# Four edits to a two-block transformer kernel: load order, a split residual tile, a shifted norm, wider convolution matmuls

## The chip, the cores and the metric

The kernel runs on one core of one Trainium2 chip. The metric is the device time of one execution in microseconds (us), the median of several executions. Lower is better. Engines are named as the profile names them: PE (TensorE matmul), PEld (TensorE weight load), DVE (VectorE), ACT (ScalarE), POOL (GpSimd), SP (SyncE, which here only issues DMAs).

## What is computed

Two blocks of two layers each work on 256 tokens of width 1024 in float32. In the first block a layer is a mixer (gated linear attention beside retention) and a feed-forward part (a SwiGLU of width 2816, then eight experts). In the second block a context of 256 further tokens runs beside the first 256. Its first layer is SwiGLU, short convolution, SwiGLU; its second is SwiGLU, latent attention, SwiGLU. Every part is preceded by an RMS norm that is scaled and shifted by "modulations", which are products of a condition vector with large matrices:

```python
def rms_norm_2(x, g):
    y = x * rsqrt(mean(x * x, axis=-1) + EPS)
    return y * g

def pre(h, g, shift, scale):
    return rms_norm_2(h, g) * (1 + scale) + shift

def adaln_chunks(cond, w_mod, b_mod):              # 9 vectors of 1024 (6 in the first block)
    return split(silu(cond) @ w_mod + b_mod, N_MOD)

def short_conv_mixer(h, w_in, conv_w, w_out):      # 3 taps along the tokens, centred
    b_gate, c_gate, u = split(h @ w_in, 3, axis=-1)
    return (b_gate * conv3_centred(c_gate * u, conv_w)) @ w_out
```

In the second block's first layer the convolution runs on the 256 tokens and on the 256 of the context, so on 512 columns.

## The kernel before, in words

**Layout and precision.** Activations stand transposed: 128 rows of the width on the partitions, eight such blocks (KD = 8), tokens along the free axis. Every float32 product is made of three matmuls on parts `hi` and `lo` of both operands (`dot_w`, lines 523 to 527: hi·hi at L525, lo·hi at L526, hi·lo at L527). The residual stream is the tile `H`, 128 x 8 x 512: columns 0 to 255 are the tokens, 256 to 511 the context.

**The stream of loads.** Class `Stream` (line 44) plans everything that SP loads through five buffers of 1 MB (tile `raw`, 128 x 2048). A *weight unit* (DRAM tensor `in_wts`) is loaded, cast to `whi` by ACT (L117), and DVE subtracts to get `wlo` (L121). There are three pairs of those, and a unit is split up to two steps ahead of the step that multiplies with it. A *modulation unit* (DRAM tensor `in_modt`) is not split: at its own step DVE multiplies it by the condition vector and sums each row (`column`, L280, two halves of 1024 columns, each once or, in the second block's first five vectors, twice). Steps run in program order, and every engine works its queue strictly in the order in which the steps were written. The order of the loads is a list of its own, `seq`; a unit that is appended with `after=n` is put into that list only behind the next n weight units. In the kernel before all units have n = 0, so the loads stand in the order of the steps.

`act` (line 329) appends a weight step and, by a rate that is set for each part, calls `fill`, which appends one modulation step ahead of it:

```python
key, src, fn = queue.pop(0)
S.step([(src, False)], fn)
```

The rate is 0.75 in the first mixer, 0.88 in the first feed-forward part (`ffn_a`), 0 in the experts, and between 0.45 and 0.8 later.

**The start.** SP loads the tokens (L1909), then modulation units 0 to 2, two weight units, and units 3 to 7. ACT squares the eight blocks of `H` and PE sums them (`first_stats`); DVE takes the inverse root. The first norm's scale and shift arrive in eight pieces, one for each block k: `cols(k)` is two columns and a small operation that makes `A` (L801). `go(k)` then has ACT scale the block (L816) and cast it to `ahi` (L817), DVE make `alo` (L818), and PE multiply block k by the first two weight units.

**The convolution.** For each quarter m2 of the width, `conv` multiplies by three units `c`, `u` and `b` of 256 columns. `products` runs over blocks kc, token halves h and column blocks j, so each matmul has 256 token columns; the accumulator is one bank for each half h. The first `c` and `u` (m2 = 0) are interleaved with the norm's blocks and run a half at a time. The evacuation (`out_c`, `out_u`, `out_b`) works by halves too.

Of the kernel before, what the change touches and what calls it, by code (L numbers as in the profile page):

```python
# [208 lines left out]
def body(ctx: ExitStack, tc: tile.TileContext, A: dict, out: bass.AP):  # L209
# [107 lines left out]
    def fill(n):  # L317
        for _ in range(min(n, len(queue))):
            while queue[0][1] is None:
                S.step([], queue.pop(0)[2])  # L320
            key, src, fn = queue.pop(0)
            S.step([(src, False)], fn)

    def need(key):

# [15 lines left out]
        S.step([], fn)  # L341


    H = cst.tile([128, KD, 512], F32, name="H")

    def rsqrt_ops(ms, n):

# [37 lines left out]
    class Stat:  # L385


        def __init__(self, off):
            self.off = off
            self.s = slice(off, off + TOK)  # L390
            self.pend = self.R = None

        def add(self, m):
            src = H[:, m, self.s]
# [42 lines left out]
        def modulate(self, hi, lo, a, b):  # L437

            def finish(m, t):
                nc.scalar.activation(hi[:, m, self.s], t, AF.Identity, bias=b[:, m:m + 1])  # L440
                nc.vector.scalar_tensor_tensor(lo[:, m, self.s], t, b[:, m:m + 1], hi[:, m, self.s].bitcast(F32),
                                               op0=OP.add, op1=OP.subtract)

            ts = []
            for m in range(KD):
                t = T()[:, :TOK]
                nc.vector.scalar_tensor_tensor(t, H[:, m, self.s], a[:, m:m + 1], self.R[:, :TOK], op0=OP.mult, op1=OP.mult)
                ts.append(t)
                if m == 0:
                    finish(0, t)  # L450
                    yield 0
                elif m > 1:
                    finish(m - 1, ts[m - 1])
                    yield m - 1
            finish(KD - 1, ts[KD - 1])
            yield KD - 1

    class Final(Stat):
# [8 lines left out]
        def add(self, m):  # L467
            for scale in (1.0, vc("final_g", m)):
                sq = T()[:, :TOK]
                nc.scalar.activation(sq, H[:, m, self.s], AF.Square, scale=scale)  # L470
                self.sq.append(sq)

        def take(self):
# [31 lines left out]

        def done(self):
            for m in range(KD):
                nc.vector.scalar_tensor_tensor(H[:, m, self.s], H[:, m, self.s], vc("final_g", m), self.acc2,
                                               op0=OP.mult, op1=OP.mult)

    def scale_cols(key, g, sc):
# [221 lines left out]
    def resid_of(gates, stats, final=False):  # L733

        def resid(m, o, h, last=True):
            g = gates()
            for i in (range(len(g)) if h is None else [h]):
                src = o[:, half(i)] if h is None else o
                d = H[:, m, half(i)]
                nc.vector.scalar_tensor_tensor(d, src, g[i][:, m:m + 1], d, op0=OP.mult, op1=OP.add)  # L740
                if last and stats is not None:
                    stats[i].add(m)
                elif last and final:
                    nc.sync.dma_start(out[:, m], d)
        return resid


    def mixer(l, s_in, ab, resid):
# [41 lines left out]
        if l == 0:  # L790
# [14 lines left out]
            def normed(a, b):  # L805
                if a == 0:
                    xs[0] = P["p"].tile([128, 1536], F32, name="S")
                    xs[1] = P["p"].tile([128, 512], F32, name="la")
                for k in range(a, b):
                    v = xs["v", k] = xs[k // 6][:, (k % 6) * 256:(k % 6) * 256 + 256]  # L810
                    nc.vector.tensor_mul(v, H[:, k, 0:TOK], s_in.R[:, :TOK])
# [8 lines left out]
            def cols_step(j, then=None):  # L820
                def fn(raw):
                    cols(j)(raw)
                    if then is not None:
                        then()
                S.step([(A["modt"][j].rearrange("p (a b) -> p a b", a=2), False)], fn)

            def start(pa, pq):
                xs["w"] = pa, pq
                for k in range(3):
                    chunk(k)  # L830
                first_products(pa, pq, range(3))

            def go(k):
                chunk(k)
                first_products(*xs["w"], [k])
                if k == KD - 1:
                    S.free(2)
                    S.ahead(2)
                    first_out()
# [944 lines left out]
    def conv(stats, ab, resid, hook):  # L1784
# [14 lines left out]
        for m2 in range(4):  # L1799
            hold = {}  # L1800

            def products(nm, part, hs, kcs, hold=hold):
                whi, wlo = part
                for kc in kcs:
                    for h in hs:
                        for j in range(2):
                            dot_w(hold[nm, h][:, half(j)], whi[:, kc, blk(j)], wlo[:, kc, blk(j)],
                                  st["a"][0][:, kc, half(h)], st["a"][1][:, kc, half(h)],
                                  first=(kc == 0 and j == 0), last=(kc == KD - 1))

            def alloc(nm, hold=hold):
                for h in range(2):
                    hold[nm, h] = bank()

            def out_c(hold=hold):
                for h in range(2):
                    hold["cs", h] = T()
                    nc.scalar.copy(hold["cs", h], hold["c", h])

            def out_u(m2=m2, hold=hold):  # L1820
                for h in range(2):
                    cu = m["cu"][h]
                    nc.vector.tensor_mul(cu[:, :, 1:257], hold["cs", h].rearrange("p (j t) -> p j t", j=2),
                                         hold["u", h].rearrange("p (j t) -> p j t", j=2))
                    y = hold["y", h] = T()
                    for j in range(2):
                        v = y[:, half(j)]
                        wc = lambda tap: vc("sc_conv_2", tap * 8 + 2 * m2 + j)
                        nc.scalar.activation(v, cu[:, j, 1:257], AF.Copy, scale=wc(1))
                        nc.vector.scalar_tensor_tensor(v, cu[:, j, 0:256], wc(0), v, op0=OP.mult, op1=OP.add)  # L1830
                        nc.vector.scalar_tensor_tensor(v, cu[:, j, 2:258], wc(2), v, op0=OP.mult, op1=OP.add)

            def out_b(m2=m2, hold=hold):
                for h in range(2):
                    y = hold["y", h]
                    nc.vector.tensor_mul(y, y, hold["b", h])
                    split_to(st["g"][0][:, 2 * m2:2 * m2 + 2, half(h)], st["g"][1][:, 2 * m2:2 * m2 + 2, half(h)],
                             y.rearrange("p (j t) -> p j t", j=2))

            def unit(nm, m2=m2):  # L1840
                c0 = {"b": 0, "c": D, "u": 2 * D}[nm] + m2 * 256
# [2 lines left out]
            if m2 == 0:  # L1844
                def fn(pc_, pu, alloc=alloc, products=products, out_c=out_c, out_u=out_u):
# [2 lines left out]

                    def mm_half(h, kcs):
                        for kc in kcs:  # L1850
                            products("c", pc_, [h], [kc])
                            products("u", pu, [h], [kc])
                    entry_of(st, stats, ab)(mm_half)
                    out_c()
                    out_u()
# [1 line left out]
            else:  # L1857
                def fc(part, alloc=alloc, products=products, out_c=out_c):
                    alloc("c")
                    products("c", part, range(2), range(KD))  # L1860
                    out_c()

                def fu(part, alloc=alloc, products=products, out_u=out_u):
                    alloc("u")
                    products("u", part, range(2), range(KD))
                    out_u()
                act([unit("c")], fc)
                act([unit("u")], fu)

            def fb(part, alloc=alloc, products=products, out_b=out_b):  # L1870
                alloc("b")
                products("b", part, range(2), range(KD))
# [33 lines left out]
        return hook  # L1906


    nc.sync.dma_start(H[:, :, 0:TOK], A["xt"])  # L1909
    s_a = Stat(0)  # L1910

    def first_stats():
        s_a.p = tbank()
        for k in range(KD):
            sq = T()[:, :TOK]
            nc.scalar.activation(sq, H[:, k, 0:TOK], AF.Square)
# [228 lines left out]
```

## Time and profile before

| What | Value |
|---|---|
| Median of three runs | 2718.47 us (2715.21 to 2720.2) |
| The profiled execution's own time | 2725.84 us |
| Its span | 2724.0 us, 36201 instructions |
| PE busy | 2578.3 us (95%) |
| DVE busy | 1806.8 us (66%) |
| ACT busy | 1088.1 us (40%) |
| DMA | 511.46 MB, mean 188 GB/s |
| Chain that ended last | PE 73% of the span, in lines L525 to L527 alone 54% |

The span runs from the first to the last instruction; 1.84 us of the execution's time lie outside it. The profiled execution was 7.4 us (0.27%) longer than the median of the runs. A matmul's duration in the trace includes a pipeline's depth, so consecutive matmuls overlap in it: how fast they follow each other is read from their starts.

### The profile page before, as it was taken

How to read it: one execution, taken by the hardware profiler on the slowest of the kernel's cores; microseconds unless marked ns; L12 is line 12 of the kernel's file. 1: busy time of each engine (PE TensorE's matmuls, PEld its weight loads, DVE VectorE, ACT ScalarE, POOL GpSimd, SP SyncE). 2: the span in 40 equal slices, each digit the busy share in tenths (PEclk: the TensorE clock that was granted, in tenths of full speed). 3: DMA queues.
4: the chain of work that ended last, by engine and by line, in shares of the span. 5: the costliest groups of instructions: out<-in, count | busy, mean ns of one | idle time of the engine just before them, and what ended most of it. 6: DMA issues, size and time to landing. Idle time of an engine off the chain costs nothing.

```text
span 2724.0 us, 36201 instructions
## 1 busy us (share of the span) xinstructions
PE 2578.3 (95%) x15060; PEld 2277.0 (84%) x15060; DVE 1806.8 (66%) x2477; ACT 1088.1 (40%) x1214; POOL 25.9 (1%) x40
## 2 busy tenths in 40 slices
PE   5988998978999999999999999999999999999999
PEld 4778987777888888888889998888888888876999
DVE  5867777776888886655558766555476654555653
ACT  3433335346777775222223233222232122345442
POOL 0100000000000000000000000000000000000000
PEclk6999998888999999999999999999999999999999
DMA  7655886435988984343333423443324554202442
GB/s 297 232 201 219 309 316 251 167 140 208 342 335 329 350 331 176 141 167 133 126 144 125 170 109 139 153 149 135 136 109 166 201 190 176 79 32 78 173 177 100
DMA packets 77297, 511.46 MB, mean 188 GB/s; under 512 B 8498, under 2 KB 11860, under 8 KB 23236
## 3 DMA queue, kind: packets, MB, share of 16 engines
q1 hardware_dynamic: 76020, 506.27, 50.2%
q8 instruction: 120, 1.97, 0.3%
q0 software_dynamic: 672, 2.00, 0.2%
q10 hardware_dynamic: 432, 0.79, 0.1%
q14 instruction: 53, 0.43, 0.1%
HBM read 507.97 MB, written 1.05 MB: 187 GB/s over the span
## 4 chain that ended last, share of the span: by engine, by line
PE 73%; DVE 2%; ACT 1%; issue 1%; DVEq 0%; ACTq 0%
PE acc L526 18%; PE acc L525 18%; PE acc L527 18%; PE acc L532 4%; PE acc L533 4%; PE acc L531 4%; DVE wlo L121 1%; PE acc L1742 1%; PE acc L1715 1%; ACT whi L117 1%; PE acc L1319 1%; PE acc L1331 1%; PE acc L1714 0%; PE tb L1360 0%; DVE accs L401 0%
## 5 line engine op out<-in xcount | busy, mean ns | idle before, releaser
L121 DVE TENSOR_TENSOR wlo<-raw,whi 128x2048 fp32r<-128x2048 f32 (+3 forms) x385 | 818.9, 2133 | 449.5 <-ACT whi L117 448.8
L117 ACT CAST whi<-raw 128x2048 fp32r<-128x2048 f32 (+3 forms) x387 | 686.8, 1782 | 718.2 <-PE acc L526 309.2
L525 PE MATMUL acc<-ahi,whi 128*128 128x256 f32 (+1 forms) x2624 | 859.0, 327 | 17.2 <-ACT ahi L817 11.5
L527 PE MATMUL acc<-ahi,wlo 128*128 128x256 f32 (+1 forms) x2624 | 855.6, 326 | 11.6 <-DVE wlo L121 11.6
L526 PE MATMUL acc<-alo,whi 128*128 128x256 f32 (+1 forms) x2624 | 857.1, 327 | 6.3 <-DVE alo L818 5.5
L525 PEld LDWEIGHTS acc<-ahi,whi 128*128 128x128 f32 x2624 | 510.1, 194 | 59.4 <-ACT ahi L817 12.8
L527 PEld LDWEIGHTS acc<-ahi,wlo 128*128 128x128 f32 x2624 | 509.8, 194 | 51.5 <-DVE wlo L121 14.0
L526 PEld LDWEIGHTS acc<-alo,whi 128*128 128x128 f32 x2624 | 510.0, 194 | 47.1 <-DVE alo L818 6.6
L526 PE MATMUL acc<-glo,whi 128*128 128x256 f32 (+1 forms) x1076 | 346.9, 322 | 0.0
L527 PE MATMUL acc<-ghi,wlo 128*128 128x256 f32 (+1 forms) x1044 | 338.7, 324 | 6.3 <-DVE wlo L121 6.2
L525 PE MATMUL acc<-ghi,whi 128*128 128x256 f32 (+1 forms) x1044 | 338.8, 324 | 0.0
L280 DVE CUSTOM_DVE_ANT_0 raw<-raw,cond,vec 128x1024 f32<-128x1024 f32 x240 | 303.8, 1286 | 15.6 <-DMA raw<-in_modt_dram 11.5
L527 PEld LDWEIGHTS acc<-ghi,wlo 128*128 128x128 f32 x1044 | 199.1, 191 | 23.4 <-DVE wlo L121 7.9
L526 PEld LDWEIGHTS acc<-glo,whi 128*128 128x128 f32 x1076 | 205.1, 191 | 15.6
L525 PEld LDWEIGHTS acc<-ghi,whi 128*128 128x128 f32 x1044 | 199.2, 191 | 15.6
L536 ACT CAST ghi<-T 128x512 fp32r<-128x512 f32 x88 | 54.7, 622 | 339.6 <-DVE T L610 339.6
L610 DVE TENSOR_TENSOR T<-T,acc 128x512 f32<-128x512 f32 x88 | 60.3, 685 | 153.8 <-PE acc L527 153.8
L531 PE MATMUL acc<-whi,xg 128*128 128x512 f32 (+1 forms) x384 | 145.9, 380 | 0.0
L280 DVE CUSTOM_DVE_ANT_0 T<-raw,cond,vec 128x1024 bf16<-128x1024 f32 x112 | 143.3, 1280 | 1.7 <-ACT cond L269 1.7
L533 PE MATMUL acc<-whi,xg 128*128 128x512 f32 (+1 forms) x384 | 144.4, 376 | 0.0
L532 PE MATMUL acc<-wlo,xg 128*128 128x512 f32 (+1 forms) x384 | 144.3, 376 | 0.0
L537 DVE TENSOR_TENSOR glo<-T,ghi 128x512 fp32r<-128x512 f32 x88 | 60.9, 692 | 60.5 <-ACT ghi L536 60.5
(370 smaller groups left out, 2432.7 us busy)
## 6 DMA issues: line engine op xcount, KB each, us to landing
raw<-in_wts_dram SPq DMA_DIRECT2D x300, 1024.0 KB, 5.0
raw<-in_modt_dram SPq DMA_DIRECT2D x120, 1024.0 KB, 4.8
raw<-in_wts_dram SPq DMA_DIRECT2D x60, 768.0 KB, 4.6
raw<-in_wts_dram SPq DMA_DIRECT2D x18, 512.0 KB, 3.7
raw<-in_wts_dram SPq DMA_DIRECT2D x2, 896.0 KB, 5.4
dec<-in_consts_dram SPq DMA_DIRECT2D x2, 768.0 KB, 6.7
raw<-in_mla_w_uq_dram SPq DMA_DIRECT2D x2, 768.0 KB, 4.2
H<-in_xt_dram SPq DMA_DIRECT2D x1, 1024.0 KB, 9.1
```

The source lines that it names most:

```text
L117: nc.scalar.copy(hd, sv)
L121: nc.vector.tensor_sub(ld, sv, hd.bitcast(F32))
L280: nc.vector.tensor_tensor_reduce(w if last else T().bitcast(mybir.dt.bfloat16), w, cond, 1.0, bias, OP.mult, OP.add, out)
L525: mm(o, whi, xhi, start=first, stop=False, skip_group_check=True)
L526: mm(o, whi, xlo, start=False, stop=False, skip_group_check=True)
L527: mm(o, wlo, xhi, start=False, stop=last, skip_group_check=True)
L531: mm(o, xhi, whi, start=first, stop=False, skip_group_check=True)
L532: mm(o, xhi, wlo, start=False, stop=False, skip_group_check=True)
L533: mm(o, xlo, whi, start=False, stop=last, skip_group_check=True)
L536: nc.scalar.copy(hi, v)
L537: nc.vector.tensor_sub(lo, v, hi.bitcast(F32))
L610: nc.vector.tensor_mul(v, s, b3[:, :n])
```

## The change

Four things are edited.

1. `fill` appends modulation units with `after=2`: each is loaded behind two weight units that are used after it. The step itself stays where it was.
2. `H` becomes two tiles of 128 x 8 x 256, one for the tokens and one for the context. All uses are renamed; the two loads that fill them are now written in one run of 2048 columns for each partition instead of eight runs of 256.
3. In the first norm `alo` and the products of block k - 1 (`use`) are written behind the scaling and cast of block k.
4. In `conv`, `products` runs over column blocks j, then blocks kc, with all 512 token columns in one matmul (except for the first `c` and `u`). An accumulator bank now belongs to a column block j, and the evacuation works by j.

```diff
@@ fill
-            S.step([(src, False)], fn)
+            S.step([(src, False)], fn, after=2)
...
-    H = cst.tile([128, KD, 512], F32, name="H")
+    H = [cst.tile([128, KD, TOK], F32, name=f"H{i}") for i in range(2)]
...
@@ mixer, first norm
             def chunk(k):
-                t = T()[:, :TOK]
-                hi, lo = st["a"][0][:, k], st["a"][1][:, k]
+                t = xs["t", k] = T()[:, :TOK]
                 nc.scalar.activation(t, xs["v", k], AF.Identity, scale=A_[:, k:k + 1], bias=sh[:, k:k + 1])
-                nc.scalar.copy(hi, t)
-                nc.vector.tensor_sub(lo, t, hi.bitcast(F32))
+                nc.scalar.copy(st["a"][0][:, k], t)
+
+            def use(k):
+                nc.vector.tensor_sub(st["a"][1][:, k], xs["t", k], st["a"][0][:, k].bitcast(F32))
+                first_products(*xs["w"], [k])
...
                 for k in range(3):
                     chunk(k)
-                first_products(pa, pq, range(3))
+                for k in range(2):
+                    use(k)
             def go(k):
                 chunk(k)
-                first_products(*xs["w"], [k])
+                use(k - 1)
                 if k == KD - 1:
+                    use(k)
                     S.free(2)
...
@@ conv
-                for kc in kcs:
-                    for h in hs:
-                        for j in range(2):
-                            dot_w(hold[nm, h][:, half(j)], whi[:, kc, blk(j)], wlo[:, kc, blk(j)],
-                                  st["a"][0][:, kc, half(h)], st["a"][1][:, kc, half(h)],
-                                  first=(kc == 0 and j == 0), last=(kc == KD - 1))
+                for j in range(2):
+                    for kc in kcs:
+                        dot_w(hold[nm, j][:, toks], whi[:, kc, blk(j)], wlo[:, kc, blk(j)],
+                              st["a"][0][:, kc, toks], st["a"][1][:, kc, toks],
+                              first=(kc == 0 and toks.start == 0), last=(kc == KD - 1))
...
-                    for j in range(2):
-                        v = y[:, half(j)]
-                        wc = lambda tap: vc("sc_conv_2", tap * 8 + 2 * m2 + j)
-                        nc.scalar.activation(v, cu[:, j, 1:257], AF.Copy, scale=wc(1))
-                        nc.vector.scalar_tensor_tensor(v, cu[:, j, 0:256], wc(0), v, op0=OP.mult, op1=OP.add)
-                        nc.vector.scalar_tensor_tensor(v, cu[:, j, 2:258], wc(2), v, op0=OP.mult, op1=OP.add)
+                    v = y.rearrange("p (h t) -> p h t", h=2)
+                    wc = lambda tap: vc("sc_conv_2", tap * 8 + 2 * m2 + j)
+                    nc.scalar.activation(v, cu[:, :, 1:257], AF.Copy, scale=wc(1))
+                    nc.vector.scalar_tensor_tensor(v, cu[:, :, 0:256], wc(0), v, op0=OP.mult, op1=OP.add)
+                    nc.vector.scalar_tensor_tensor(v, cu[:, :, 2:258], wc(2), v, op0=OP.mult, op1=OP.add)
...
-                            products("c", pc_, [h], [kc])
+                            products("c", pc_, half(h), [kc])
...
-                    products("c", part, range(2), range(KD))
+                    products("c", part, slice(0, 512), range(KD))
...
-    nc.sync.dma_start(H[:, :, 0:TOK], A["xt"])
+    nc.sync.dma_start(H[0], A["xt"])
...
-        nc.sync.dma_start(H[:, :, TOK:2 * TOK], A["ctxt"])
+        nc.sync.dma_start(H[1], A["ctxt"])
```

**SP's loads as `ffn_a` begins.** Before (the number in a name only tells tiles apart):

```order
L97 DMA raw_1723<-in_wts_dram 128x2048
L97 DMA raw_1725<-in_modt_dram 128x2048
L97 DMA raw_1782<-in_wts_dram 128x2048
L97 DMA raw_1784<-in_modt_dram 128x2048
L97 DMA raw_1847<-in_wts_dram 128x2048
L97 DMA raw_1849<-in_modt_dram 128x2048
L97 DMA raw_1906<-in_wts_dram 128x2048
```

DVE, in the same place before, takes those buffers in this order (the rows between are other operations):

```order
L121 TENSOR_TENSOR wlo_1852<-raw_1847,whi_1851 128x2048
L280 ISA raw_1725,mod1_0_5_1720<-raw_1725,cond0_76,vec_86 128x1024
L121 TENSOR_TENSOR wlo_1911<-raw_1906,whi_1910 128x2048
L280 ISA raw_1784,mod1_1_0_1969<-raw_1784,cond0_76,vec_86 128x1024
L121 TENSOR_TENSOR wlo_1977<-raw_1972,whi_1976 128x2048
```

So the modulation unit `raw_1725`, loaded ahead of the weights `raw_1782` and `raw_1847`, is used up behind `raw_1847`. With the change, SP loads:

```order
L97 DMA raw_1711<-in_wts_dram 128x2048
L97 DMA raw_1717<-in_modt_dram 128x2048
L97 DMA raw_1732<-in_wts_dram 128x2048
L97 DMA raw_1734<-in_modt_dram 128x2048
L97 DMA raw_1787<-in_wts_dram 128x2048
L97 DMA raw_1793<-in_modt_dram 128x2048
L97 DMA raw_1852<-in_wts_dram 128x2048
```

and DVE uses them in this order:

```order
L121 TENSOR_TENSOR wlo_1790<-raw_1711,whi_1789 128x2048
L280 ISA raw_1717,mod1_0_5_1729<-raw_1717,cond0_76,vec_86 128x1024
L121 TENSOR_TENSOR wlo_1855<-raw_1732,whi_1854 128x2048
L280 ISA raw_1734,mod1_0_5_1729<-raw_1734,cond0_76,vec_86 128x1024
L121 TENSOR_TENSOR wlo_1914<-raw_1787,whi_1913 128x2048
L280 ISA raw_1793,mod1_1_0_1974<-raw_1793,cond0_76,vec_86 128x1024
L121 TENSOR_TENSOR wlo_1980<-raw_1852,whi_1979 128x2048
```

DVE's work stands in the same order as before, apart from three weight subtractions in the whole program that come a few rows earlier; the loads now stand in the order in which DVE gives their buffers back. In the whole program each modulation unit that `fill` appends (units 8 to 119) stands two weight units later in SP's list.

**DVE in the first norm.** Before, around block 3 (`T_251` is that block):

```order
L280 ISA raw_173,mod1_0_1_93<-raw_173,cond0_76,vec_86 128x1024
L280 ISA mod1_0_1_93 128x1
L801 SCALAR_TENSOR_TENSOR A_100_94<-mod1_0_1_93,vec_86 128x1
L818 TENSOR_TENSOR alo_110<-T_251,ahi_109 128x256
L280 ISA raw_184,mod1_0_0_92<-raw_184,cond0_76,vec_86 128x1024
```

With the change (`T_214` is block 2):

```order
L280 ISA raw_174,mod1_0_1_94<-raw_174,cond0_76,vec_86 128x1024
L280 ISA mod1_0_1_94 128x1
L803 SCALAR_TENSOR_TENSOR A_100_95<-mod1_0_1_94,vec_86 128x1
L822 TENSOR_TENSOR alo_111<-T_214,ahi_110 128x256
L280 ISA raw_185,mod1_0_0_93<-raw_185,cond0_76,vec_86 128x1024
```

The `alo` behind the columns of block 3 is that of block 2.

## Rows read from the trace of the kernel before

**Rows 1.** Page part 1: busy time, share of the span and instructions of each engine.

```profile
PE 2578.3 (95%) x15060; PEld 2277.0 (84%) x15060; DVE 1806.8 (66%) x2477; ACT 1088.1 (40%) x1214; POOL 25.9 (1%) x40
```

**Rows 2.** Windows by stage: first mixer, `ffn_a`, convolution (columns in its first line).

```profile
core 0: us, PE busy (x) PEld busy (x) DVE busy (x) ACT busy (x) POOL busy (x), PEclk, DMA share, GB/s
52.00:225.00 173.00, 147.15 (x926) 131.85 (x926) 124.23 (x211) 73.46 (x90) 7.55 (x9) 0.90 0.53 199
225.00:420.00 195.00, 182.05 (x1481) 178.44 (x1481) 151.55 (x172) 71.87 (x59) 0.00 (x0) 1.00 0.81 303
...
1424.00:1620.00 196.00, 192.24 (x1503) 186.86 (x1503) 149.93 (x262) 63.02 (x88) 1.00 (x2) 1.00 0.38 144
```

**Rows 3.** Waits, 225 to 420 us: total, times, longest.

```profile
ACT whi L117 <- DMA raw<-in_wts_dram: 82.6, 21, 6.9
...
PE acc L527 <- DVE wlo L121: 12.8, 16, 1.5
```

**Rows 4.** Timelines of SP, ACT, DVE and PE, 246 to 258 us: start, duration, instruction.

```profile
246.64 1.28 DVE L280 CUSTOM_DVE_ANT_0 raw<-raw,cond,vec 128x1024 f32<-128x1024 f32 x1
...
247.95 0.33 SPq L97 DMA_DIRECT2D raw<-in_wts_dram  x1
...
253.46 1.91 ACT L117 CAST whi<-raw 128x2048 fp32r<-128x2048 f32 x1 [6.86 <-DMA raw<-in_wts_dram]
...
255.40 2.29 DVE L121 TENSOR_TENSOR wlo<-raw,whi 128x2048 fp32r<-128x2048 f32 x1 [2.86 <-ACT whi L117]
...
257.75 0.39 PE L527 MATMUL acc<-ahi,wlo 128*128 128x256 f32 x1 [1.55 <-DVE wlo L121]
```

**Rows 5.** Groups by line, DVE, 225 to 420 us: busy, mean ns | idle before.

```profile
L280 DVE CUSTOM_DVE_ANT_0 raw<-raw,cond,vec 128x1024 f32<-128x1024 f32 x56 | 69.6, 1279 | 0.0
L121 DVE TENSOR_TENSOR wlo<-raw,whi 128x2048 fp32r<-128x2048 f32 x29 | 66.4, 2289 | 35.7 <-ACT whi L117 35.7
```

**Rows 6.** DMA issues of page part 6: KB each, median us to landing.

```profile
raw<-in_modt_dram SPq DMA_DIRECT2D x120, 1024.0 KB, 4.8
...
H<-in_xt_dram SPq DMA_DIRECT2D x1, 1024.0 KB, 9.1
```

**Rows 7.** Timeline of DVE at the start.

```profile
12.48 1.28 DVE L280 CUSTOM_DVE_ANT_0 raw<-raw,cond,vec 128x1024 f32<-128x1024 f32 x1 [11.48 <-DMA raw<-in_modt_dram]
...
16.65 0.16 DVE L424 TENSOR_SCALAR ms<-tb 128x2 f32<-128x2 f32 x1 [1.48 <-PE tb L1918]
```

**Rows 8.** Timeline of DVE in the first norm, blocks 3 to 7.

```profile
34.56 0.42 DVE L818 TENSOR_TENSOR alo<-T,ahi 128x256 fp32r<-128x256 f32 x1 [1.17 <-ACT ahi L817]
34.90 1.28 DVE L280 CUSTOM_DVE_ANT_0 raw<-raw,cond,vec 128x1024 f32<-128x1024 f32 x1
...
37.43 0.16 DVE L801 SCALAR_TENSOR_TENSOR A<-mod,vec 128x1 f32<-128x1 f32 x1
38.75 0.42 DVE L818 TENSOR_TENSOR alo<-T,ahi 128x256 fp32r<-128x256 f32 x1 [1.16 <-ACT ahi L817]
39.09 1.28 DVE L280 CUSTOM_DVE_ANT_0 raw<-raw,cond,vec 128x1024 f32<-128x1024 f32 x1
...
51.15 0.42 DVE L818 TENSOR_TENSOR alo<-T,ahi 128x256 fp32r<-128x256 f32 x1 [1.10 <-ACT ahi L817]
```

**Rows 9.** Timeline of PE in the convolution (256 columns) and its output (512 columns).

```profile
1470.81 0.28 PE L526 MATMUL acc<-alo,whi 128*128 128x256 f32 x1
...
1479.93 0.28 PE L527 MATMUL acc<-ahi,wlo 128*128 128x256 f32 x1
...
1570.75 0.40 PE L525 MATMUL acc<-chi,whi 128*128 128x512 f32 x1
...
1579.83 0.39 PE L526 MATMUL acc<-clo,whi 128*128 128x512 f32 x1
```

**Rows 10.** Windows in the second mixer and at the start (columns as in rows 2).

```profile
510.00:520.00 10.00, 10.00 (x36) 8.64 (x37) 5.68 (x10) 4.15 (x5) 0.00 (x0) 0.50 0.55 210
...
8.00:20.00 12.00, 6.75 (x34) 6.31 (x34) 5.70 (x18) 3.93 (x9) 0.00 (x0) 0.96 1.03 418
```

More of the change, by code (lines that the diff above doesn't have):

```diff
@@ L390, in __init__ @@
             self.s = slice(off, off + TOK)
+            self.H = H[off // TOK]
             self.pend = self.R = None
         def add(self, m):
-            src = H[:, m, self.s]
+            src = self.H[:, m]
             if m == 0:
@@ L738, in resid @@
                 src = o[:, half(i)] if h is None else o
-                d = H[:, m, half(i)]
+                d = H[i][:, m]
                 nc.vector.scalar_tensor_tensor(d, src, g[i][:, m:m + 1], d, op0=OP.mult, op1=OP.add)
@@ L810, in normed, with cols_step @@
                     v = xs["v", k] = xs[k // 6][:, (k % 6) * 256:(k % 6) * 256 + 256]
-                    nc.vector.tensor_mul(v, H[:, k, 0:TOK], s_in.R[:, :TOK])
+                    nc.vector.tensor_mul(v, H[0][:, k], s_in.R[:, :TOK])
             def chunk(k):
-                t = T()[:, :TOK]
-                hi, lo = st["a"][0][:, k], st["a"][1][:, k]
+                t = xs["t", k] = T()[:, :TOK]
                 nc.scalar.activation(t, xs["v", k], AF.Identity, scale=A_[:, k:k + 1], bias=sh[:, k:k + 1])
-                nc.scalar.copy(hi, t)
-                nc.vector.tensor_sub(lo, t, hi.bitcast(F32))
-            def cols_step(j, then=None):
+                nc.scalar.copy(st["a"][0][:, k], t)
+            def use(k):
+                nc.vector.tensor_sub(st["a"][1][:, k], xs["t", k], st["a"][0][:, k].bitcast(F32))
+                first_products(*xs["w"], [k])
+            def cols_step(j, then):
                 def fn(raw):
                     cols(j)(raw)
-                    if then is not None:
-                        then()
+                    then()
                 S.step([(A["modt"][j].rearrange("p (a b) -> p a b", a=2), False)], fn)
@@ L1800, in conv, with products @@
             hold = {}
[L1802 removed]
+            def products(nm, part, toks, kcs, hold=hold):
                 whi, wlo = part
[L1804 to L1809 removed]
+                for j in range(2):
[3 more added lines that the diff above has]
+                              first=(kc == 0 and toks.start == 0), last=(kc == KD - 1))
@@ L1811, in alloc @@
             def alloc(nm, hold=hold):
-                for h in range(2):
-                    hold[nm, h] = bank()
+                for j in range(2):
+                    hold[nm, j] = bank()
             def out_c(hold=hold):
-                for h in range(2):
-                    hold["cs", h] = T()
-                    nc.scalar.copy(hold["cs", h], hold["c", h])
+                for j in range(2):
+                    hold["cs", j] = T()
+                    nc.scalar.copy(hold["cs", j], hold["c", j])
@@ L1833, in out_b @@
-            def out_b(m2=m2, hold=hold):
[L1834 to L1838, printed above, removed]
+                for j in range(2):
+                    cu = m["cu"][j]
+                    nc.vector.tensor_mul(cu[:, :, 1:257], hold["cs", j].rearrange("p (h t) -> p h t", h=2),
+                                         hold["u", j].rearrange("p (h t) -> p h t", h=2))
+                    y = hold["y", j] = T()
+                    v = y.rearrange("p (h t) -> p h t", h=2)
[3 more added lines that the diff above has]
+                    nc.vector.scalar_tensor_tensor(v, cu[:, :, 2:258], wc(2), v, op0=OP.mult, op1=OP.add)
@@ L1840, in unit @@
+            def out_b(m2=m2, hold=hold):
+                for j in range(2):
+                    y = hold["y", j]
+                    nc.vector.tensor_mul(y, y, hold["b", j])
+                    split_to(st["g"][0][:, 2 * m2 + j], st["g"][1][:, 2 * m2 + j], y)
             def unit(nm, m2=m2):
@@ L1850, in mm_half @@
                         for kc in kcs:
-                            products("c", pc_, [h], [kc])
-                            products("u", pu, [h], [kc])
+                            products("c", pc_, half(h), [kc])
+                            products("u", pu, half(h), [kc])
                     entry_of(st, stats, ab)(mm_half)
@@ L1864, in fu @@
                     alloc("u")
-                    products("u", part, range(2), range(KD))
+                    products("u", part, slice(0, 512), range(KD))
                     out_u()
@@ L1871, in fb @@
                 alloc("b")
-                products("b", part, range(2), range(KD))
+                products("b", part, slice(0, 512), range(KD))
                 out_b()
@@ L1915, in first_stats @@
             sq = T()[:, :TOK]
[L1916 removed]
+            nc.scalar.activation(sq, H[0][:, k], AF.Square)
             for t in range(2):
```

11 lines of the change are left out of this document (3 added, 8 removed).

## The prediction, made before the change was run

> **What bounds the kernel now.** I read the page's busy shares first, then windows by stage, then in each stage the wait that ends last, and last the starts of single instructions. PE is busy for 95% of the span [rows 1], so 2724.0 - 2578.3 = 145.7 us are all that better feeding can give back; more has to come from PE's own work. The windows tell where those lie [rows 2]: PE idles 25.9 of 173 us in the first mixer, 12.9 of 195 in `ffn_a`, and only 3.8 of 196 in the convolution. So the edit to the convolution can gain only by making PE's work shorter, and the others only where PE or the engine that feeds it waits: at the start and in `ffn_a`.
>
> **Load order (edit 1).** In `ffn_a` all of PE's waiting has one name, the weights' `lo` part: 12.8 us in 16 waits [rows 3]. Behind it stands a chain, seen once in the timelines [rows 4]: DVE finishes a modulation column at 247.9 (246.64 + 1.28); SP, which had been waiting for that buffer, issues a weight load at 247.95; ACT casts it the moment it lands, at 253.46; DVE subtracts at 255.40; PE, 1.55 us idle, goes on at 257.75. ACT waits 82.6 us for weight loads in this stage [rows 3]. The order listings say why: the modulation unit is loaded ahead of two weight units but used up behind the second, so it keeps a buffer too long, and the load that gets it is the very next one needed. With the change the loads stand in the order in which DVE gives buffers back, and a load is issued five places ahead of its use instead of just ahead of it.
>
> What is late next there? DVE is busy 151.55 of 195 us [rows 2], 28 modulation units (56 column sums, 69.6 us) and 29 weights (66.4 us) being most of it [rows 5]; with 12 us less it would be at 83%. DMA is busy 0.81 at 303 GB/s [rows 2]; the same bytes in 183 us are 323 GB/s, and the queue moved 418 GB/s over 12 us at the start [rows 10]. Neither is full. I take **-12.0 us**: 12.8 less one wait that may remain as the stage starts. Ends: 0 (something else holds the buffers) and -12.8. Elsewhere the order changes nothing I can price: the experts load no modulation units, and in the later stages PE is never idle for weights.
>
> **The token load (edit 2).** `H` takes 9.1 us to land, against a median of 4.8 for modulation units, which are the same 1 MB in one run for each partition [rows 6]. What waits for it: DVE starts its first column at 12.48, when the unit behind `H` in the same queue lands, and then idles 1.48 us for the sums over `H` [rows 7]. If `H` landed at the median, 4.3 us would go; if the unit behind it came no earlier, 1.48. The queue is full from 8 us on [rows 10], so bytes set the pace and I stay near the lower: **-2.0 us**, ends 0 and -4.3. The Trainium skill ("DMA: Bandwidth & Descriptors", Specifications) has runs of 512 bytes and more at line rate, and `H` had runs of 1 KB; by that the term would be 0 and the sum below -23.1. The rows don't contradict it, since `H` shared its first microseconds with other queues. The other part of the split, separate tiles, frees no wait: none in the trace is on the other half of `H`.
>
> **The shifted norm (edit 3).** From block 3 on DVE's chain has a period of 39.09 - 34.90 = 4.19 us, and in each it stands still until ACT has scaled and cast the block that DVE's own `A` just released: 1.17, 1.16, 1.10, 1.10 and 1.10 us [rows 8], where the first, second and last are shown. Now the subtraction of the block before fills that place, and four of the five waits go; the last stays, shortened by one subtraction (39.09 - 38.75 = 0.34). 5.63 - 1.10 + 0.34 = **-4.9 us**. The period becomes 4.19 - 1.1 = 3.1 us, so units 3 to 7 are wanted sooner. A transfer takes 1.05 MB / 418 GB/s = 2.5 us [rows 10], less than the period, so DVE should not wait for them. Ends: -2.5 (half is lost to late units) and -5.6.
>
> Do these 6.9 us last? DVE's queue is in order and carries the first mixer from there (busy 124 of 173 us, [rows 2]), waiting in turn for ACT and PE, which move with it. The weights that come next are now loaded ahead of modulation units, so none should be later. I count it whole.
>
> **The convolution (edit 4).** Of 12 weight units, the first two stay at 256 columns; ten lose half of their 96 matmuls, so 960 of 256 columns become 480 of 512. Durations mislead here, since they overlap, so I take starts [rows 9]: 77 matmuls of 256 columns from 1470.81 to 1479.93 are 9.12 / 76 = 0.1200 us each; 41 of 512 columns from 1570.75 to 1579.83 are 9.08 / 40 = 0.2270. A pair of the first costs 0.2400. 480 x 0.0130 = **-6.2 us**. It lies on the path, as PE is idle 3.8 us in that stage, and DVE (149.9 of 196 us) loses 16 operations besides. Ends: 0 and -6.5. The Trainium skill ("TensorE: Matmul & The Clock Gate", Back-to-back issue gap) gives N/2.4 + 2.5 ns between single matmuls, so 109.2 and 215.8, a gain of 2.5 ns for each pair: an estimate from that page is -1.2 us in place of -6.2 and -20.1 for the sum. The rows show 120.0 and 227.0 here, and they decide.
>
> **The sum.** -12.0 - 2.0 - 4.9 - 6.2 = -25.1 us on the profiled execution's own 2725.84, which gives 2700.7. That execution lay 7.4 us above the median of the runs shown, 2718.47; against that median it is 2693.4. I forecast **2693 us**. A measurement of this kernel tells about 0.2%, 5.4 us, from no change.
>
> **The rivals.**
>
> *The clock in the second mixer.* From 510 to 520 us PE is busy throughout, but at a granted 0.50 (1.2 GHz) [rows 10], after a gap in its work while DVE caught up; it lasts some 14 us and costs about 7. Loads that come sooner could close the gap. For it: ACT waits for weights there too. Against: DVE has almost no idle time just before, and its order is unchanged. -25 - 7 gives 2686. Chance 0.10. The reverse, a gap that now opens in the first mixer, at +7, gives 2700. Chance 0.06.
>
> *`ffn_a` keeps part of its waits.* If DVE's in-order queue, ACT, or the transport sets the pace at 0.88 modulation units for each weight, half or all of the 12 us stays: 2699 to 2705. For it: DVE at 83% in a stage whose pieces are 2.3 us long. Against: nothing but the load stands in the chain of [rows 4]. Chance 0.14.
>
> *Matmuls of 512 columns gain next to nothing*, so that a pair at 256 and one at 512 cost the same but for a few nanoseconds: 2698. The page of the Trainium skill on TensorE, above, would have it so; [rows 9] speak against it. Chance 0.02.
>
> *The change does little of what it says.* The buffers are given back in another order than I read, `H` lands no sooner, and only the shifted norm and part of the convolution come through: 2713 or more, within 0.2% of before. The order listings speak against it. Chance 0.03.
>
> *Slower: DVE waits for late modulation units.* They are now loaded later, and a DVE queue that stops at one holds the weights behind it. If each of `ffn_a`'s 28 came in only one load ahead, it would be waited for 4.8 us [rows 6] less the 2.3 us of the weight that DVE works on meanwhile [rows 5], 2.5 us x 28 = 70; DVE's 43 idle us of the stage take up the rest, so the stage is 27 us longer instead of 12 shorter: about 2732. It decides when a modulation unit's load is issued less than 4.8 us before DVE reaches it. Against: with five buffers and equal orders it is issued about two and a half weights ahead, 14 us at 5.7 us for each. Chance 0.03.
>
> **How the numbers follow.** My forecast, the sum give or take 4 us for the ends of its terms, has the rest, 0.62. The range 2683 to 2706 takes in that, both clock cases and the kept waits of `ffn_a`; it leaves out no change, slower, and the tails. Faster by over 0.2% are the forecast, both clock cases, the kept waits and the matmul case: 0.94. Within 0.2% is the case of little effect, 0.03; slower the last, 0.03.
>
> **What would show it.** In the profile after: PE's waits for `wlo` in `ffn_a` near 0 and ACT's for weight loads there well under 20 us; `H` landing in under 8 us and the first column before 12; the `alo` waits gone from all blocks of the first norm but the last, and a period of 3.1 us; 480 fewer matmuls, with 0.227 us between starts in the convolution, and its stage 6 us shorter. If DVE shows waits on `in_modt` beyond the first, edit 1 was misread. If the stage ends are earlier but the total is not, the clock took it back.

## The result, and the profile after

The changed kernel takes 2694.13 us (2690.54 to 2696.31, four runs) against 2718.81 us before (2715.21 to 2720.2, four runs): a ratio of 0.991, interval 0.9893 to 0.9927, so 24.7 us less. Timed once more beside other kernels (the run `e6_again` below), it took 2691.27 against 2719.11, a ratio of 0.9891 (0.9874 to 0.9907). The forecast was 2693. It holds, but two of its four terms were off, in opposite directions.

The profile after is of the run of 2690.54 us, the shortest of its four, while the one before was of a run of 2725.84 us, 7.0 above the median of 2718.81. The two profiles therefore differ by 35.3 us, 10.6 more than the medians do, and the whole spans are no measure of the change. Stages are. Lines of the changed kernel stand up to 6 higher in number: the three matmuls of `dot_w` are L527 to L529, `alo` of the first norm is L822, its `A` L803, and the first use of the sums is L426.

Page part 1 of the kernel after, to be held against [rows 1]: busy time, share of the span and instructions of each engine.

```profile
PE 2556.8 (95%) x14580; PEld 2242.2 (83%) x14580; DVE 1803.1 (67%) x2461; ACT 1086.0 (40%) x1206; POOL 26.0 (1%) x40
```

There are 480 matmuls fewer and 21.5 us less of PE's busy time, and DVE has lost 3.7 us: PE was and remains the bound. Not all of the 21.5 us is the change's doing: the profile of the split alone, whose PE does the same 15060 matmuls as before, has 2570.1 us, 8.2 less, at a mean granted clock of 0.972 instead of 0.968.

To see where the time went, take a landmark that every kernel here has, the start of DVE's n-th weight subtraction. It comes from the timeline of DVE (start, duration, instruction, idle before it). Before, the 1st and 3rd (around the first norm), the 25th and 56th (around `ffn_a`), the 254th and 281st (around the convolution):

```profile
26.36 1.22 DVE L121 TENSOR_TENSOR wlo<-raw,whi 128x1024 fp32r<-128x1024 f32 x1
...
52.95 2.29 DVE L121 TENSOR_TENSOR wlo<-raw,whi 128x2048 fp32r<-128x2048 f32 x1 [1.38 <-ACT whi L117]
...
241.24 2.29 DVE L121 TENSOR_TENSOR wlo<-raw,whi 128x2048 fp32r<-128x2048 f32 x1 [2.16 <-ACT whi L117]
...
440.70 2.29 DVE L121 TENSOR_TENSOR wlo<-raw,whi 128x2048 fp32r<-128x2048 f32 x1 [1.31 <-ACT whi L117]
...
1419.43 2.29 DVE L121 TENSOR_TENSOR wlo<-raw,whi 128x2048 fp32r<-128x2048 f32 x1 [9.23 <-ACT whi L117]
...
1734.51 2.29 DVE L121 TENSOR_TENSOR wlo<-raw,whi 128x2048 fp32r<-128x2048 f32 x1 [1.12 <-ACT whi L117]
```

The same six after:

```profile
26.25 1.22 DVE L121 TENSOR_TENSOR wlo<-raw,whi 128x1024 fp32r<-128x1024 f32 x1
...
47.61 2.29 DVE L121 TENSOR_TENSOR wlo<-raw,whi 128x2048 fp32r<-128x2048 f32 x1 [1.38 <-ACT whi L117]
...
233.64 2.29 DVE L121 TENSOR_TENSOR wlo<-raw,whi 128x2048 fp32r<-128x2048 f32 x1
...
416.60 2.29 DVE L121 TENSOR_TENSOR wlo<-raw,whi 128x2048 fp32r<-128x2048 f32 x1 [1.31 <-ACT whi L117]
...
1389.32 2.29 DVE L121 TENSOR_TENSOR wlo<-raw,whi 128x2048 fp32r<-128x2048 f32 x1 [9.23 <-ACT whi L117]
...
1697.99 2.29 DVE L121 TENSOR_TENSOR wlo<-raw,whi 128x2048 fp32r<-128x2048 f32 x1 [1.12 <-ACT whi L117]
```

Differences of these starts give the stages. Up to the first weights nothing is gained (26.36 and 26.25). The first norm takes 21.36 us instead of 26.59, `ffn_a` 182.96 instead of 199.46, the stretch with the convolution 308.67 instead of 315.08. That is 5.2 + 16.5 + 6.4 = 28.1 us; of the 7.2 us that are left, 4.6 lie in one place where the granted clock differs too, as the last section shows.

**`ffn_a`.** Its window after (columns in the first line), to be held against the second row of [rows 2]:

```profile
core 0: us, PE busy (x) PEld busy (x) DVE busy (x) ACT busy (x) POOL busy (x), PEclk, DMA share, GB/s
218.00:401.00 183.00, 180.65 (x1506) 180.44 (x1504) 155.80 (x177) 73.21 (x60) 1.63 (x3) 1.00 0.90 342
```

PE idles 2.35 us of 183 instead of 12.95 of 195. DVE is at 85%, and the queues move 342 GB/s. The waits in that window (total, times, longest):

```profile
ACT whi L117 <- PE acc L528: 48.4, 14, 5.3
DVE wlo L121 <- ACT whi L117: 18.9, 8, 5.4
ACT whi L117 <- DMA raw<-in_wts_dram: 7.8, 3, 4.4
```

ACT's waits for weight loads fall from 82.6 to 7.8 us, and PE no longer has a row for `wlo` [rows 3]. What ACT waits for now is PE, which has to give back the pair of `whi` and `wlo`: the chain is turned round, and the loads are ahead of the engine that bounds.

**The first norm.** DVE's timeline, the `alo` of blocks 4 to 7, to be held against [rows 8]:

```profile
38.74 0.42 DVE L822 TENSOR_TENSOR alo<-T,ahi 128x256 fp32r<-128x256 f32 x1
...
41.68 0.42 DVE L822 TENSOR_TENSOR alo<-T,ahi 128x256 fp32r<-128x256 f32 x1
...
44.62 0.42 DVE L822 TENSOR_TENSOR alo<-T,ahi 128x256 fp32r<-128x256 f32 x1
...
45.81 0.43 DVE L822 TENSOR_TENSOR alo<-T,ahi 128x256 fp32r<-128x256 f32 x1 [0.77 <-ACT ahi L818]
```

Each block takes 2.94 us instead of 4.19, and only the last `alo` waits, which has no column in front of it.

**The convolution.** PE's timeline in it, to be held against the first two rows of [rows 9]: the first and the last of six matmuls of 512 columns.

```profile
1509.77 0.39 PE L527 MATMUL acc<-ahi,whi 128*128 128x512 f32 x1
...
1510.90 0.39 PE L529 MATMUL acc<-ahi,wlo 128*128 128x512 f32 x1
```

Five steps in 1.13 us are 0.226 each, where a pair of 256 columns took 0.240.

**The start.** The first loads before (KB each, us from issue to landing; the row for `H` is in [rows 6]):

```profile
cond<-in_c_dram ACTq DMA_DIRECT2D x1, 512.0 KB, 4.5
...
vec<-in_vecs_dram ACTq DMA_DIRECT2D x1, 192.0 KB, 9.1
```

and after:

```profile
H<-in_xt_dram SPq DMA_DIRECT2D x1, 1024.0 KB, 7.2
...
cond<-in_c_dram ACTq DMA_DIRECT2D x1, 512.0 KB, 6.6
...
vec<-in_vecs_dram ACTq DMA_DIRECT2D x1, 192.0 KB, 12.2
```

`H` lands 1.9 us sooner, as wanted. But the two loads that ACT's queue issues at the same time land 2.1 and 3.1 us later, and `vec` is an operand of every modulation column. DVE's first column after, against the first row of [rows 7]:

```profile
13.93 1.28 DVE L280 CUSTOM_DVE_ANT_0 raw<-raw,cond,vec 128x1024 f32<-128x1024 f32 x1 [12.92 <-DMA vec<-in_vecs_dram]
...
16.54 0.15 DVE L426 TENSOR_SCALAR ms<-tb 128x2 f32<-128x2 f32 x1
```

The column waits for `vec` and starts 1.45 us later; the 1.48 us of waiting behind it, for the sums over `H`, are gone. One cancels the other.

### The profile page after: what moved, and what is told of

The parts are those of the page before. It is cut to its first block, busy times and chain, and to the rows that moved or that the text cites. A ratio compares the mean times of both kernels' runs of the same rounds, so it can differ in the third digit from the quotient of the medians.

```text
span 2688.7 us, 35218 instructions
## 1 busy us (share of the span) xinstructions
PE 2556.8 (95%) x14580; PEld 2242.2 (83%) x14580; DVE 1803.1 (67%) x2461; ACT 1086.0 (40%) x1206; POOL 26.0 (1%) x40
## 4 chain that ended last, share of the span: by engine, by line
PE 74%; DVE 3%; ACT 1%; issue 0%; DVEq 0%; ACTq 0%
PE acc L528 18%; PE acc L529 18%; PE acc L527 18%; PE acc L534 4%; PE acc L535 4%; PE acc L533 4%; DVE wlo L121 1%; PE acc L1748 1%; ACT whi L117 1%; PE acc L1325 1%; PE acc L1721 1%; PE acc L1337 1%; PE acc L1720 0%; PE tb L1366 0%; DVE accs L403 0%
## 5 line engine op out<-in xcount | busy, mean ns | idle before, releaser
L528 PE MATMUL acc<-alo,whi 128*128 128x256 f32 (+1 forms) x2464 | 827.9, 336 | 13.0 <-DVE alo L822 12.3
L527 PE MATMUL acc<-ahi,whi 128*128 128x256 f32 (+1 forms) x2464 | 829.1, 336 | 10.0 <-ACT ahi L442 4.4
L529 PE MATMUL acc<-ahi,wlo 128*128 128x256 f32 (+1 forms) x2464 | 825.3, 335 | 5.3 <-DVE wlo L121 5.3
L528 PEld LDWEIGHTS acc<-alo,whi 128*128 128x128 f32 x2464 | 478.1, 194 | 60.5 <-DVE alo L822 13.4
L527 PEld LDWEIGHTS acc<-ahi,whi 128*128 128x128 f32 x2464 | 478.3, 194 | 57.5 <-ACT ahi L442 6.3
L529 PEld LDWEIGHTS acc<-ahi,wlo 128*128 128x128 f32 x2464 | 477.9, 194 | 49.0 <-DVE wlo L121 5.7
L527 PE MATMUL acc<-ghi,whi 128*128 128x256 f32 (+1 forms) x1044 | 338.6, 324 | 0.0
L529 PE MATMUL acc<-ghi,wlo 128*128 128x256 f32 (+1 forms) x1044 | 337.7, 323 | 0.0
L527 PEld LDWEIGHTS acc<-ghi,whi 128*128 128x128 f32 x1044 | 199.2, 191 | 15.8
L529 PEld LDWEIGHTS acc<-ghi,wlo 128*128 128x128 f32 x1044 | 199.0, 191 | 15.3
```

The source lines that it names most:

```text
L527: mm(o, whi, xhi, start=first, stop=False, skip_group_check=True)
L528: mm(o, whi, xlo, start=False, stop=False, skip_group_check=True)
L529: mm(o, wlo, xhi, start=False, stop=last, skip_group_check=True)
```

## The experiments

**Each part alone.** Four kernels, each the kernel before with one of the four edits.

```diff
@@ e1_order: fill
-            S.step([(src, False)], fn)
+            S.step([(src, False)], fn, after=2)
```

> The kernel before with edit 1 alone (modulation units loaded two weight units later). Theory: the load order is what made PE wait in the first feed-forward part, so PE's waits for the lo parts there fall from 12.8 us to under 2, ACT's waits for weight loads from 83 us to under 20, and the stage gets 13 to 17 us shorter (the waits, and up to 0.2 us each to start PE's pipeline again); total about 2703 us. Rival: the waits went because of the other edits (an earlier start, the split of the residual tile), so this kernel stays within 4 us of the one before and keeps the waits.

```diff
@@ e2_split
-    H = cst.tile([128, KD, 512], F32, name="H")
+    H = [cst.tile([128, KD, TOK], F32, name=f"H{i}") for i in range(2)]
...
-    nc.sync.dma_start(H[:, :, 0:TOK], A["xt"])
+    nc.sync.dma_start(H[0], A["xt"])
...
```

> The kernel before with edit 2 alone (residual tile in two halves, tokens and context each loaded in one run per partition). Theory: the tokens land at 7.2 us instead of 9.1, but take the transfer engines' time from the vectors' load on the other queue, which lands at about 13.8 us; the first column starts at 13.9 us instead of 12.5 and the sums over the tokens no longer wait, so the first norm ends where it did (within 0.5 us) and the total is within 2 us of before. Rival, as forecast: the first column starts before 12 us and the start is 2 us shorter.

```diff
@@ e3_norm
...
             def go(k):
                 chunk(k)
-                first_products(*xs["w"], [k])
+                use(k - 1)
                 if k == KD - 1:
+                    use(k)
...
```

> The kernel before with edit 3 alone (first norm shifted by a block). Theory: the period of DVE in the first norm goes from 4.19 to about 2.95 us, the last subtraction there comes 5 us sooner, and the total is about 5 us less, 2714. Rival: the gain is eaten up before the first feed-forward part starts, because DVE then waits for weights that have not landed; the last subtraction comes sooner and the total stays.

```diff
@@ e4_conv
...
-                    products("c", part, range(2), range(KD))
+                    products("c", part, slice(0, 512), range(KD))
...
```

> The kernel before with edit 4 alone (512 columns for each matmul of the convolution). Theory: starts of matmuls 0.227 us apart instead of 0.120, 480 instructions fewer, the stage 6.2 us shorter, total about 2712. Rival (single-matmul spacing by column count alone): the stage is 1 us shorter.

Measured against 2721.81 us for the kernel before, timed beside them (the last row against 2719.11), and the stages by the landmarks above:

| Kernel | us | ratio (interval) | first norm | `ffn_a` | convolution |
|---|---|---|---|---|---|
| before (profiled execution) | | | 26.59 | 199.46 | 315.08 |
| load order alone | 2703.07 | 0.9929 (0.9915 to 0.9942) | 26.61 | 182.99 | 313.89 |
| split `H` alone | 2720.7 | 1.0001 (0.9992 to 1.001) | 26.61 | 197.06 | 315.08 |
| shifted norm alone | 2718.57 | 0.9985 (0.9976 to 0.9994) | 21.37 | 197.08 | 315.10 |
| convolution alone | 2714.64 | 0.9977 (0.9966 to 0.9987) | 26.61 | 196.26 | 308.69 |
| all four, again (`e6_again`) | 2691.27 | 0.9891 (0.9874 to 0.9907) | 21.36 | 182.97 | 308.68 |

The stages agree to a few hundredths between kernels that share an edit, so each edit acts in its own place. `ffn_a` is the exception: with the old order four profiles have it between 196.26 and 199.46, mean 197.5, and with the new one it is 182.97 to 182.99. The load order is worth 13.3 to 16.5 us there, 14.5 from the mean, and about 19 us (0.71%) by its own ratio, whose interval goes from 16 to 23. Another 1.2 us of that lie right behind the stage: from the 56th to the 73rd subtraction the four profiles with the old order take 149.5 to 149.8 us, and the six with `after` at 1, 2 or 4 take 148.1 to 148.5. PE has one wait for `wlo` in there, of 1.5 us before and 0.2 after; with `after=1` (below) it is 1.5 again and the stretch is as short, so what shortens it is not shown. The split of `H` is worth nothing, the norm about 4 and the convolution about 6; in the profile of the split alone the first column starts at 14.18 us and waits for `vec`, as in the changed kernel. That the load order's profile also shows 1.2 us in the convolution is not additive: with the wider matmuls the stage is 308.7 with or without it. It goes with the clock: in that one profile the granted clock of the stretch is 1.00 throughout, while each of the others has 3.4 us at half in it (the one before from 1619.8 on).

In the profile of the load order alone, the waits from 225 to 420 us:

```profile
ACT whi L117 <- PE acc L526: 51.1, 14, 5.7
...
DVE wlo L121 <- ACT whi L117: 19.5, 8, 5.4
...
ACT whi L117 <- DMA raw<-in_wts_dram: 7.0, 4, 2.6
```

They are those of the whole change, so this one argument, `after`, does all that happens in `ffn_a`.

**All four again.**

> The changed kernel itself, unaltered, timed in more rounds. If the four parts simply add, as their own runs suggest (about 19 + 0 + 4 + 6 us), the ratio is 0.989 (about 2692 us); if parts take from each other, above all the load order and the shifted norm, the ratio stays at 0.991 or more and the interval leaves 0.989 out.

The parts' own ratios add up to 0.71 - 0.01 + 0.15 + 0.23 = 1.08%, and 1.09% was measured. This interval leaves a ratio of 0.991 just out, but the first comparison had given 0.991 itself. The stages speak for the sum: 21.36, 182.97 and 308.68 us for all four together are what each edit has alone. In these stages nothing is taken from one part by another.

**Is "two" the point of the load order?** The order listings had shown that `after=2` equals the order in which DVE gives buffers back. Two kernels, the changed one with another number:

```diff
@@ fill
-            S.step([(src, False)], fn, after=2)
+            S.step([(src, False)], fn, after=1)
```

> The changed kernel, with each modulation unit loaded behind one unit of weights instead of two. Theory (two is the order in which DVE gives the raw buffers back, so that each load goes out as its buffer comes free): part of the waits of PE for wlo in the feed-forward comes back, with ACT waits on the weight loads between 20 and 83 us in that stage, and the time is 3 to 12 us above the changed kernel. Rival (any place behind the first weights is as good): no waits, the same time within 1 us.

```diff
@@ fill
-            S.step([(src, False)], fn, after=2)
+            S.step([(src, False)], fn, after=4)
```

> The changed kernel, with each modulation unit loaded behind four units of weights. Theory (order of use decides): DVE now reaches modulation columns before their unit has landed, so waits of DVE on in_modt appear beyond the first, PE waits for wlo behind them, and the time is 5 to 20 us above the changed kernel. Rival (weights first is simply better): no such waits, the same time within 1 us or a little less.

With 1 it took 2693.82 us (ratio 0.9901, 0.9885 to 0.9918), with 4 2693.43 (0.9896, 0.9878 to 0.9914), beside 2691.27 for 2, timed together. My expectation fell for 1, as the medians differ by 2.6 us with intervals that overlap and the waits of PE stayed away; for 4 only the waits of DVE came as expected. The waits with `after=1`, 218 to 401 us:

```profile
ACT whi L117 <- DMA raw<-in_wts_dram: 44.8, 19, 4.9
...
ACT whi L117 <- PE acc L528: 26.6, 7, 5.2
```

ACT waits for loads again, 44.8 us, about half of what it was before. But no wait of PE for `wlo` follows, and `ffn_a` takes 182.97 us as with 2: the loads come with less in hand, and still in time. It isn't the equality of the two orders that counts in this stage; one place was enough. With `after=4`, in the same window:

```profile
DVE raw L280 <- DMA raw<-in_modt_dram: 18.3, 22, 3.6
...
DVE wlo L121 <- ACT whi L117: 6.3, 2, 5.1
...
PE acc L529 <- DVE wlo L121: 0.7, 2, 0.5
```

There the new wait is: DVE stands 22 times for a modulation unit, 18.3 us together. The 25th and 56th subtractions say what it costs:

```profile
235.30 2.29 DVE L121 TENSOR_TENSOR wlo<-raw,whi 128x2048 fp32r<-128x2048 f32 x1
...
422.32 2.29 DVE L121 TENSOR_TENSOR wlo<-raw,whi 128x2048 fp32r<-128x2048 f32 x1 [1.30 <-ACT whi L117]
```

187.02 us, 4.05 more than with 2. Most of the 18.3 us took the place of DVE's waits for `whi` (18.9 us with 2, 6.3 with 4). What reached PE came for the most part not through the weights, where I had expected it, but at the end of the stage, where PE waits for DVE's sums for the next norm. Its wait there with 4, and with 2:

```profile
PE tb L419 <- DVE accs L403: 6.9, 1, 6.9
...
PE tb L419 <- DVE accs L403: 4.2, 1, 4.2
```

That is 2.7 us; the two waits for `wlo`, counted from the starts of the matmuls around them, add 1.2, and the two together are 3.9 of the 4.05. On the whole time 4 us don't show: the medians differ by 2.2 and the intervals overlap, so the expected 5 to 20 us were too much.

**Did `vec` eat the gain of the split?** The changed kernel, with that load moved to SP's queue, behind `H`:

```diff
-    nc.scalar.dma_start(VT, A["vecs"])
...
     nc.sync.dma_start(H[0], A["xt"])
+    nc.sync.dma_start(VT, A["vecs"])
```

> The changed kernel with one load moved: the vector block (vec) goes out from the SP queue right behind the residual stream H instead of from the ACT queue. Theory (vec is what the first modulation column waits for, because H in long runs leaves the ACT queue a smaller share): the first DVE column starts at about 11 us instead of 13.9, the first convolution weights follow, the first norm is some 2 to 3 us earlier, and the whole is about 2.9 us shorter than the changed kernel. Rival (the start is bound by the bytes of all loads together): the column starts where it did, or the matrix M0 lands later and the gain is under 1 us.

It took 2688.65 us (ratio 0.9884, 0.9868 to 0.9901), the shortest of all, 2.6 us below the changed kernel timed beside it; the intervals overlap. The start of its DVE timeline (its lines stand one lower):

```profile
11.53 1.28 DVE L279 CUSTOM_DVE_ANT_0 raw<-raw,cond,vec 128x1024 f32<-128x1024 f32 x1 [10.52 <-DMA raw<-in_modt_dram]
...
15.30 0.16 DVE L425 TENSOR_SCALAR ms<-tb 128x2 f32<-128x2 f32 x1 [1.08 <-PE tb L1922]
...
25.01 1.22 DVE L121 TENSOR_TENSOR wlo<-raw,whi 128x1024 fp32r<-128x1024 f32 x1
```

The column starts 2.40 us sooner and waits for its modulation unit again, not for `vec`. Of that, 1.24 us reach the statistics and the first weights, since the sums over `H` are now the late ones, by 1.08 us. So it is shown that `vec` held the start up, and also that more than half of my 2.9 us was hidden behind the next wait. How much of the 2.6 us in the medians is this, and how much is chance, stays open; the profiles vouch for 1.2 at this place.

## Why the prediction held, step by step

- **The bound.** Right: PE was at 95% and is at 95%; what went is PE's own work in the convolution and its idle time in the first norm and in `ffn_a`.
- **Load order, -12.0 with a floor of -12.8.** The mechanism was right: the chain of [rows 4] is gone, PE's waits for `wlo` went from 12.8 us to none, ACT's for loads from 82.6 to 7.8 (forecast well under 20). What the prediction gave as the reason, loads in just the order in which DVE gives buffers back, is more than was needed: one place does as well as two in this stage. It also had PE "never idle for weights" later on, where the trace before has waits for `wlo` of 2.2 and 1.5 us. The term was too small; it measured 14.5 (13.3 to 16.5). The step that failed is the bound "12.8 less one wait that may remain": it took the idle time that the waits show for the whole of a stall's cost. It isn't. PE's timeline before, ahead of the wait that closes [rows 4], and behind it:

```profile
255.80 0.28 PE L525 MATMUL acc<-ahi,whi 128*128 128x256 f32 x1
255.92 0.28 PE L526 MATMUL acc<-alo,whi 128*128 128x256 f32 x1
...
257.97 0.28 PE L525 MATMUL acc<-ahi,whi 128*128 128x256 f32 x1
258.09 0.28 PE L526 MATMUL acc<-alo,whi 128*128 128x256 f32 x1
```

  Matmuls start every 0.12 us there. The stalled one should have started at 256.04 and did at 257.75; the next came 0.22 behind it instead of 0.12. That is 1.71 + 0.10 = 1.81 us for a wait listed as 1.55, because the idle time is counted from the end of a matmul (0.28) that overlaps the next. Sixteen times 0.26 are 4.2 us: 17.0 in place of 12.8, against 16.5 measured (199.46 - 182.96). Each of the other fifteen, counted from the starts in the same way, also costs 0.26 us more than is listed. The three other profiles with the old order bear it out: waits of 10.1 us in 13 (split alone), 11.1 in 16 (norm alone) and 10.5 in 14 (convolution alone) become 13.5, 15.3 and 14.1, and their stages were 14.1, 14.1 and 13.3 us longer than 182.97. No run of its own tested it, and the sums miss the stages by up to 1.2 us.
- **DVE and the queues in `ffn_a`.** Forecast: DVE at 83%, 323 GB/s. Found: 85%, 342 GB/s. Neither became the bound.
- **The token load, -2.0.** Failed; its end of 0 was the answer. `H` landed in 7.2 us as forecast ("under 8"), but "the first column before 12" was wrong: 13.93. The step had two things that the column waits for, `H` and the unit behind it, and left out a third, `vec` on another queue. By the Trainium skill ("DMA: Bandwidth & Descriptors", Specifications) the term would have been 0; 0 was measured, though not in that way, as `H` did land 1.9 us sooner in its long runs.
- **The shifted norm, -4.9.** Right: 5.2 us in its stage, period 2.94 (forecast 3.1), one wait left. By its own ratio 4 us of the total (1.6 to 6.5). The modulation units were in time.
- **The convolution, -6.2.** Right: 6.4 us in the stretch, 6.3 by its own ratio, 480 matmuls fewer, 0.226 us apart. By the formula that the prediction took from the Trainium skill ("TensorE: Matmul & The Clock Gate", Back-to-back issue gap), it would have been -1.2, an estimate; the trace doesn't agree, with 120.0 and 226 ns between starts where the formula has 109.2 and 215.8. The prediction left out that this section gives the formula for single matmuls only, and says itself that at a small N it counts too little where a weight load goes with each matmul, as here (15060 of each). That it counts too much at a large N, which the section says as well, the 226 ns don't bear out.
- **The sum.** -25.1 forecast; -14.5 + 0 - 5.2 - 6.4 = -26.1 by stages, -27.3 with the 1.2 behind `ffn_a`; 24.7 and 27.8 us between medians. The two errors, +2.5 and -2.0, nearly cancel, so the total was closer than its parts deserve, and that is luck.
- **The rivals.** The half clock in the second mixer stayed. Its window after, against the first row of [rows 10]:

```profile
480.00:494.00 14.00, 12.87 (x48) 11.07 (x49) 9.74 (x17) 3.71 (x5) 1.03 (x2) 0.51 0.50 190
```

  The granted clock is 0.51 (1.2 GHz), after the same gap: PE stands 1.72 and 1.06 us for DVE's `St` just ahead, 1.74 and 1.08 before. Kept waits in `ffn_a`, gainless wide matmuls and little effect are excluded by the stages. The slower rival, DVE waiting for late units, exists: four places bring it, two do not, and the cost of 4 us is far from the 27 that the prediction gave for the worst case.

## What to carry to other kernels

Where several kinds of loads share a ring of buffers, let the list of loads come near the order in which buffers come free, and check the spread: one or two places behind were equal here, none cost 14 us, four cost 4, all in one stage. Price a stall from the starts of the instructions around it and not from the idle time that a view lists, when the engine is pipelined. When a load is made faster, look at what was on the other queues in the same microseconds and list everything that the first instruction waits for, not only what lies in the same queue.

## What had not been expected

- One load in long runs delays its neighbours: with `H` in 8 KB runs instead of 1 KB, `H` landed in 7.2 us instead of 9.1, `cond` in 6.6 instead of 4.5 and `vec` in 12.2 instead of 9.1. In the profile of the split alone it is 7.1, 6.5 and 12.4. In the first 6 us of the span the trace has 0.57 MB in 555 packets on the queue of `H` and 0.58 MB in 264 on ACT's before, and 0.79 MB in 97 and 0.49 MB in 119 after. What makes the shares shift was not tested apart.
- Identical work differs by several microseconds from profile to profile, and the clock goes with it in part. Right after the second mixer, between the 73rd and 74th weight subtraction, the profile before takes 39.52 us (590.51 to 630.03), that of the split alone 37.10, and the changed kernel's two profiles 34.95 and 37.80. In the profile before the granted clock is at half for 23.9 us from 599.2 on, in the first of the changed kernel for 10.2 us from 575.9 on, in the second for 20.5 from 576.8 on. The clock is not all of it: over the whole stretch the granted clock is 0.65 in the profile before and 0.64 in the second of the changed kernel, which is 1.7 us shorter, and 0.75 in that of the split alone and 0.76 in the first of the changed kernel, 2.2 us apart; the rest is not explained. A single pair of profiles can be 4.6 us off at this place alone; the stages compared above lie outside it.
